# The first two projections of a two-layer encoder on unnormalised tokens, with the norm's scale in the weights and the tokens' factors at eviction

## The chip, the cores and the metric

The kernel runs on one core of one Trainium2 chip. A core has a matrix engine (TensorE; PE in the rows, and PEld for its weight loads), a vector engine (VectorE, DVE), an engine for functions and scaled copies (ScalarE, ACT), a general engine (GpSimd, POOL) and SyncE (SP), whose queue issues the DMAs here. The metric is the device time of one execution in microseconds (us).

## The reference

A trunk of two layers on 256 tokens of 1024 channels, all float32. Each layer has a token mixer and a SwiGLU FFN, with an RMSNorm before and behind each. The part that matters here:

```python
h = rms_norm(x, ln_mix_pre[l])          # x * rsqrt(mean(x*x) + eps) * gain
proj = h @ w_in[l]                      # one combined input projection
c_q, c_kv, k_pe, conv_u, r_q, r_k, r_v, r_g, gate_logits = jnp.split(proj, points, axis=-1)
y_mla = mla_branch(c_q, c_kv, k_pe, cos_m, sin_m, ...)   # norms c_q, c_kv; rotates k_pe
y_conv = conv_branch(conv_u, ...)                         # gated, width 31
y_ret = retention_branch(r_q, r_k, r_v, r_g, cos_r, sin_r, ...)
...                                     # gates, output projection, FFN
```

The first group of columns (c_q, c_kv and k_pe: 416 columns) is called the latents below; the first 512 columns of r_v are the values.

## The kernel before

**Split products.** A float32 product is made of three products of a faster format: each operand is split into a high part (a rounded copy, by ScalarE) and a low part (the rest, by VectorE), and high x high, high x low and low x high are added up in one bank. `split` does it for activations, `wunit` for a weight unit: one DMA of 416 or 512 KB into a buffer `raw` (5 of them), a copy into `whi` (9 buffers) on ScalarE (line 175), a subtraction into `wlo` (8 buffers) on VectorE (line 177). `mm3` (lines 186 to 188) issues the three products. A group of columns has four units of 256 rows each; `tok_mm` runs a unit over one block of 128 tokens (there are two), `feat_group` makes transposed outputs for both blocks at once.

**The start.** SP issues the norm's gain (one row), x block 0, two weight units, x block 1, and further units (lines 119, 120, 166, 393). Ten warm products on zeros run on TensorE meanwhile, and four instructions (line 131) that spread the gain row over 128 partitions in two banks. `first_norm` squares and sums a block (ScalarE one half, VectorE the other; lines 279, 280), POOL makes the factor rs (lines 142, 143), VectorE multiplies the tokens by rs and by the gain (line 264), TensorE transposes the normed block (line 270, two times four transposes) and `split` makes its high and low parts (lines 182, 183): the tile hT. Only then does the first product of the latents start.

**What follows.** Latents and values, each over both blocks (banks `pas` and `pvs`); the values are split at eviction into vrh and vrl. `setup_tables` makes sines and cosines of the positions (sinT, cosT) and the decay logarithms (lgt), mostly on VectorE, in buffers of the tag `half`, of which there are seven. `columns` transposes small parameter rows (prow, grow). `latent` norms a block's latents (lines 443 to 450, into cn) and rotates the key part into kpad (lines 378 to 383), which needs the tables; its inner function transposes cn and kpad on TensorE (lines 460, 461). Meanwhile TensorE goes on with the conv projections, four feature groups of 48 products each.

**What sets the order.** Each engine runs its instructions in a fixed list. The list is made when the program is built: a scheduler places ready instructions by priority (the order of the code) and its own estimate of times; waits between engines are semaphores. Nothing is reordered on the chip.

```python
def wunit(src, k, c):
    ...
    raw = wraw(src, k, c)[:, :n]
    S.copy(hi, raw)
    V.tensor_sub(lo, raw, hi.bitcast(F32))
```

Of the kernel before, what the change touches and what calls it, by code (L numbers as in the profile page):

```python
# [8 lines left out]
F32 = mybir.dt.float32  # L9
# [7 lines left out]
P = 128  # L17
# [9 lines left out]
NHI = 9  # L27
NLO = 8
NRAW = 5
WARM = 10  # L30
FFN = 2816
FT = FFN // P
EPS = 1e-6
# [25 lines left out]
def tile_hybrid_encoder(  # L59
# [44 lines left out]
    def mid(name):  # L104
        return act.tile([P, 1024], F32, tag="mid", name=name, bufs=5)
# [4 lines left out]
    def acc():  # L110
        return pacc.tile([P, 512], F32, tag="acc", name="acc")

    def tp():
        return ptp.tile([P, 512], F32, tag="tp", name="tp")


    xs = cst.tile([P, NB, D], F32, tag="xs", name="xs")
    grow1 = mid("grow1")
    nc.sync.dma_start(grow1[0:1, :], ln_mix_pre[0:1, :])
    nc.sync.dma_start(xs[:, 0, :], x[0, 0:P, :])  # L120
    ones = cst.tile([1, P], F32, tag="ones", name="ones")
# [4 lines left out]
    gfirst = [acc() for _ in range(2)]  # L126
# [37 lines left out]
    def wraw(src, k, c):  # L164
        raw = wp.tile([P, 1024], F32, tag="raw", name="raw", bufs=NRAW)
        nc.sync.dma_start(raw[:, :k * c].rearrange("p (k c) -> p k c", k=k),
                          src.rearrange("(k p) c -> p k c", p=P))
        return raw

    def wunit(src, k, c):  # L170

        n = k * c
        raw = wraw(src, k, c)[:, :n]
        hi = hi_tile()[:, :n]
        S.copy(hi, raw)  # L175
# [81 lines left out]
        duals.append(t)  # L257
        return t[:, :, :SEQ], t[:, :, SEQ:]

    def pre_norm(b, hn, ss, gain, hT):  # L260
        rs = sm.tile([P, 1], F32, tag="rs", name="rs")
        rsqrt_sum(rs, ss)
# [11 lines left out]
        return transposes  # L274

    def first_norm(b, gain, hT):
        hn = mid("hn")
        ss = sm.tile([P, 2], F32, tag="ss2", name="ss2")
        S.activation(hn[:, :512], xs[:, b, :512], AF.Square, scale=1.0 / 32.0, accum_out=ss[:, 0:1])
        V.scalar_tensor_tensor(hn[:, 512:], xs[:, b, 512:], 1.0 / D, xs[:, b, 512:],  # L280
                               op0=ALU.mult, op1=ALU.mult, accum_out=ss[:, 1:2])
        pre_norm(b, hn, ss, gain, hT)()

    def boundary(b, banks, gpost, gpre, hT):

# [102 lines left out]

    def a_unit(win, i):
        return wunit(win[2 * i * P:(2 * i + 2) * P, C_A:C_CONV], 2, C_CONV)  # L390
    first_norm(0, gfirst, hT)
    ua = [a_unit(w_in[0], i) for i in range(2)]
    nc.sync.dma_start(xs[:, 1, :], x[0, P:2 * P, :])
    first_norm(1, gfirst, hT)

    for l in range(DEPTH):
        win = w_in[l]


        if l == 0:  # L400
# [3 lines left out]
        uv = [wunit(win[2 * i * P:(2 * i + 2) * P, C_RV:C_RV + 512], 2, 512) for i in range(4)]  # L404

        gqkv = half("gqkv")[:, :QR + KVR]
        nc.sync.dma_start(gqkv[:, :QR], mla_q_norm[l].partition_broadcast(P))
# [57 lines left out]
                      pc[:, :3 * P].rearrange("p (j n) -> p j n", j=3))  # L465
            return f

        pas = [acc() for _ in range(NB)]
        pvs = [acc() for _ in range(NB)]
        for c, b in ((0, 0), (0, 1), (1, 0), (1, 1)) if l == 0 else ((0, 0), (1, 0), (0, 1), (1, 1)):  # L470
# [508 lines left out]
```

## Time and profile before

| | |
|---|---|
| three runs | 936.09, 936.37 (median), 939.99 us |
| profiled execution | 939.36 us, span of its rows 937.0 us |
| TensorE busy | 925.5 us, 99% of the span |
| VectorE busy | 694.5 us, 74% |
| ScalarE busy | 535.1 us, 57% |

Rows of the timeline give start, busy time of the row, engine, line, operation, the shape of the output and input, and the count; in brackets the idle time ahead of the row on its engine and what ended it. Products are pipelined: one of 0.35 us can start every 0.188 us, so that a price is read from start to start. The page's line PEclk, and the column PEclk of the windows, give the share of full clock (2.4 GHz) that was granted; 0.50 is 1.2 GHz.

### The profile page before, as it was taken

The numbers are of one execution on the slowest core, as the hardware profiler recorded it, in microseconds if no ns is written. First come the engines' busy times: TensorE is split into PE (matmuls) and PEld (weight loads), VectorE is DVE, ScalarE is ACT, GpSimd is POOL, SyncE is SP. The second block draws the span as 40 slices with busy tenths as digits, with TensorE's granted clock in tenths as the row PEclk, the third lists the DMA queues.
The fourth block names the chain that finished last, engine by engine and source line by source line (L and its number), as shares of the span: only waits on it lengthen the run. The fifth ranks groups of instructions, "written<-read, shape, count | busy, mean of one in ns | idle before, by whom it ended". The sixth has DMA issues, their size and how long they took to land.

```text
span 937.0 us, 13295 instructions
## 1 busy us (share of the span) xinstructions
PE 925.5 (99%) x4924; PEld 787.9 (84%) x4924; DVE 694.5 (74%) x1101; ACT 535.1 (57%) x821; POOL 35.9 (4%) x77
## 2 busy tenths in 40 slices
PE   8999999999999999999999999999999999999997
PEld 6999878888887888888889998788888888888885
DVE  6789999996658776664486899999766677667532
ACT  5775886544545666553365758755454555666431
POOL 1000000000010000000120000010000100000000
PEclk7999999999999999999999999999999999999999
DMA  6785455566636766565366655645755376666621
GB/s 226 245 254 160 147 163 179 144 194 181 182 91 236 252 182 191 193 198 187 98 203 199 197 152 166 196 135 162 197 172 179 125 233 200 194 182 185 203 85 45
DMA packets 113214, 166.70 MB, mean 178 GB/s; under 512 B 5929, under 2 KB 62905, under 8 KB 113150
## 3 DMA queue, kind: packets, MB, share of 16 engines
q1 hardware_dynamic: 113150, 165.87, 57.8%
q8 instruction: 38, 0.62, 0.3%
q14 instruction: 26, 0.21, 0.1%
HBM read 164.80 MB, written 1.05 MB: 177 GB/s over the span
## 4 chain that ended last, share of the span: by engine, by line
PE 94%; ACT 2%; DVE 2%; DMA 1%; issue 0%; POOL 0%; DVEq 0%; SPq 0%; POOLq 0%; ACTq 0%
PE acc L186 22%; PE acc L188 22%; PE acc L187 22%; PE acc L241 13%; PE acc L239 7%; PE acc L238 2%; PE tp L613 1%; PE tp L649 1%; DMA raw<-in_ffn_w_up_dram 1%; PE tp L638 1%; PE tp L679 1%; DVE wlo L177 1%; PE tp L270 1%; ACT whi L175 1%; ACT qT L564 0%; DMA raw<-in_w_in_dram 0%
## 5 line engine op out<-in xcount | busy, mean ns | idle before, releaser
L175 ACT CAST whi<-raw 128x1024 fp32r<-128x1024 f32 (+1 forms) x300 | 312.2, 1049 | 226.9 <-PE acc L188 133.4
L177 DVE TENSOR_TENSOR wlo<-raw,whi 128x1024 fp32r<-128x1024 f32 (+1 forms) x300 | 362.6, 1216 | 106.0 <-PE acc L187 60.6
L241 PE MATMUL acc<-hT,whi 128*128 128x512 f32 x504 | 179.8, 397 | 0.0
L186 PE MATMUL acc<-whi,hT 128*128 128x512 f32 (+1 forms) x416 | 168.2, 404 | 0.4 <-ACT hT L182 0.4
L188 PE MATMUL acc<-whi,hT 128*128 128x512 f32 (+1 forms) x416 | 162.6, 391 | 1.0 <-DVE hT L183 0.8
L187 PE MATMUL acc<-wlo,hT 128*128 128x512 f32 (+1 forms) x416 | 162.4, 390 | 0.0
L239 PE MATMUL acc<-hT,wlo 128*128 128x256 f32 x576 | 149.1, 279 | 0.0
L239 PEld LDWEIGHTS acc<-hT,wlo 128*128 128x128 f32 x576 | 108.7, 189 | 6.2
L241 PEld LDWEIGHTS acc<-hT,whi 128*128 128x128 f32 x504 | 94.8, 188 | 19.5
L521 DVE SCALAR_TENSOR_TENSOR cacc<-apad,ccol,cacc 128x256 f32<-128x256 f32 x240 | 108.0, 476 | 1.3
L188 PEld LDWEIGHTS acc<-whi,hT 128*128 128x128 f32 x416 | 78.7, 189 | 18.7 <-DVE hT L183 2.8
L186 PEld LDWEIGHTS acc<-whi,hT 128*128 128x128 f32 x416 | 78.9, 190 | 17.9 <-issue 3.1
L187 PEld LDWEIGHTS acc<-wlo,hT 128*128 128x128 f32 x416 | 79.0, 190 | 13.7
L186 PE MATMUL acc<-hT,whi 128*128 128x256 f32 x256 | 73.5, 287 | 0.5 <-ACT kT L564 0.5
L188 PE MATMUL acc<-hT,wlo 128*128 128x256 f32 x256 | 72.5, 283 | 0.0
L187 PE MATMUL acc<-hT,whi 128*128 128x256 f32 x256 | 72.5, 283 | 0.0
L186 PE MATMUL acc<-whi,hidh 128*128 128x512 f32 x176 | 68.6, 390 | 0.0
L188 PE MATMUL acc<-whi,hidl 128*128 128x512 f32 x176 | 68.6, 389 | 0.0
L187 PE MATMUL acc<-wlo,hidh 128*128 128x512 f32 x176 | 68.5, 389 | 0.0
L186 PEld LDWEIGHTS acc<-hT,whi 128*128 128x128 f32 x256 | 49.1, 192 | 1.5 <-ACT kT L564 1.4
L187 PEld LDWEIGHTS acc<-hT,whi 128*128 128x128 f32 x256 | 49.1, 192 | 0.1
L188 PEld LDWEIGHTS acc<-hT,wlo 128*128 128x128 f32 x256 | 49.1, 192 | 0.0
(236 smaller groups left out, 1269.0 us busy)
## 6 DMA issues: line engine op xcount, KB each, us to landing
raw<-in_w_in_dram SPq DMA_DIRECT2D x112, 512.0 KB, 4.2
raw<-in_ffn_w_gate_dram SPq DMA_DIRECT2D x44, 512.0 KB, 4.5
raw<-in_ffn_w_up_dram SPq DMA_DIRECT2D x44, 512.0 KB, 4.5
raw<-in_ffn_w_down_dram SPq DMA_DIRECT2D x44, 512.0 KB, 4.6
raw<-in_ret_w_o_dram SPq DMA_DIRECT2D x16, 512.0 KB, 3.7
raw<-in_w_out_dram SPq DMA_DIRECT2D x16, 512.0 KB, 3.5
raw<-in_mla_w_o_dram SPq DMA_DIRECT2D x8, 512.0 KB, 4.7
raw<-in_conv_w_pw_dram SPq DMA_DIRECT2D x8, 512.0 KB, 3.4
```

Source lines behind the costliest of these rows:

```text
L175: S.copy(hi, raw)
L177: V.tensor_sub(lo, raw, hi.bitcast(F32))
L186: T.matmul(o, lh, rh, start=start, stop=False)
L187: T.matmul(o, lh, rl, start=False, stop=False)
L188: T.matmul(o, ll, rh, start=False, stop=stop)
L238: T.matmul(ps, wh, both[:, k, :], start=True, stop=False)
L239: T.matmul(ps[:, SEQ:], wl, both[:, k, :SEQ], start=False, stop=False)
L241: T.matmul(ps, wh, both[:, k, :], start=False, stop=k == KT - 1)
L270: T.transpose(ps[:, j * P:(j + 1) * P], hn[:, (4 * c + j) * P:(4 * c + j + 1) * P], ident)
L521: V.scalar_tensor_tensor(cacc[:, j, :], src, ccol[:, j, w:w + 1], cacc[:, j, :], op0=ALU.mult, op1=ALU.add)
L613: T.matmul(ps[:, j * SEQ:(j + 1) * SEQ], qT[:QK, 2 * pr + j, b * P:(b + 1) * P], kT[:QK, 2 * pr + j, :], start=True, stop=True)
L638: T.transpose(pt[:, jk * P:(jk + 1) * P], pe[:, jk * P:(jk + 1) * P], ident)
```

## The change

The first two groups of layer 0 (latents and values) take the tokens as they are. Since the norm is x times a factor per token times a gain per channel, the gain can go into the weights' rows and the factor into the output's rows. `g8` loads the gain as 8 rows of 128, one transpose makes of it eight columns `pcol`. `plain_T` transposes raw tokens and splits them into the tile `u` (uTh, uTl). `scaled_unit` stands for `wunit`: ScalarE copies each of the unit's two row blocks with a scale per partition, VectorE makes the low part with one fused operation each. The latents' banks are copied to `sa` with the token's factor, and the values are multiplied by it when they are split. The old norm with hT is still made, for all that follows, now with a broadcast gain tile and behind the values' splits. `Line` chains the instructions of the start on TensorE, ScalarE and VectorE in the order of the code. WARM goes from 10 to 7, and one warm product (`keep_busy(1)`) stands later.

```diff
-WARM = 10
+WARM = 7
...
-    grow1 = mid("grow1")
-    nc.sync.dma_start(grow1[0:1, :], ln_mix_pre[0:1, :])
     nc.sync.dma_start(xs[:, 0, :], x[0, 0:P, :])
-    ones = cst.tile([1, P], F32, tag="ones", name="ones")
-    V.memset(ones, 1.0)
+    g8 = act.tile([KT, P], F32, tag="grow", name="g8")
+    nc.sync.dma_start(g8, ln_mix_pre[0].rearrange("(k p) -> k p", p=P))
...
-    for i in range(WARM):
-        T.matmul(pw, warm[:, :P], warm, start=True, stop=True)
-        if i == 3:
-            for c in range(2):
-                T.matmul(gfirst[c], ones, grow1[0:1, c * 512:(c + 1) * 512], start=True, stop=True)
+    def keep_busy(n):
+        for _ in range(n):
+            inPE(T.matmul(pw, warm[:, :P], warm, start=True, stop=True))
+    keep_busy(WARM)
...
+    def plain_T(b, c, u):
+        ps = tp()
+        for j in range(4):
+            inPE(T.transpose(ps[:, j * P:(j + 1) * P], xs[:, b, (4 * c + j) * P:(4 * c + j + 1) * P], ident))
+        hi, lo = (t[:, 4 * c:4 * c + 4, b * P:(b + 1) * P] for t in u)
+        pv = ps.rearrange("p (j n) -> p j n", j=4)
+        inACT(S.copy(hi, pv))
+        return lambda: inDVE(V.tensor_sub(lo, pv, hi.bitcast(F32)))
+
+    def scaled_unit(src, k0, c, col, line=True):
...
+        for k in range(2):
+            inACT(S.activation(hi[:, k, :], raw[:, k, :], AF.Copy, scale=col[:, k0 + k:k0 + k + 1]))
+        for k in range(2):
+            inDVE(V.scalar_tensor_tensor(lo[:, k, :], raw[:, k, :], col[:, k0 + k:k0 + k + 1],
+                                         hi[:, k, :].bitcast(F32), op0=ALU.mult, op1=ALU.subtract))
+        return hi, lo
...
-    first_norm(0, gfirst, hT)
-    ua = [a_unit(w_in[0], i) for i in range(2)]
-    nc.sync.dma_start(xs[:, 1, :], x[0, P:2 * P, :])
-    first_norm(1, gfirst, hT)
+    def fast_first(pas):
+        pg = tp()
+        inPE(T.transpose(pg[:, :KT], g8, ident[:KT, :KT]))
+        col = act.tile([P, KT], F32, tag="gcol", name="pcol")
+        inDVE(V.tensor_copy(col, pg[:, :KT]))
...
+        def products(i, b, what):
+            o = pas[b][:, :C_CONV]
+            for k in range(2):
+                t = u[what == "lh"][:, 2 * i + k, b * P:(b + 1) * P]
+                inPE(T.matmul(o, t, units[i][what == "hl"][:, k, :], start=i == 0 and k == 0 and what == "hh",
+                              stop=i == 3 and k == 1 and what == "hl"))
+        lo = plain_T(0, 0, u)
+        lo()
+        unit(0)
+        lo = plain_T(0, 1, u)
+        lo()
+        nc.sync.dma_start(xs[:, 1, :], x[0, P:2 * P, :])
+        keep_busy(1)
+        products(0, 0, "hh")
+        products(0, 0, "lh")
+        for c in range(2):
+            plain_T(1, c, u)()
+        products(0, 0, "hl")
+        for what in ("hh", "lh", "hl"):
+            products(0, 1, what)
+        for i in range(1, 4):
+            unit(i)
+            for b in range(NB):
+                for what in ("hh", "lh"):
+                    products(i, b, what)
+            for b in range(NB):
+                products(i, b, "hl")
+        return u, col
...
         if l == 0:
-            ua += [a_unit(win, i) for i in range(2, 4)]
+            uT, pcol = fast_first(pas)
+            uv = [scaled_unit(win[2 * i * P:(2 * i + 2) * P, C_RV:C_RV + 512], 2 * i, 512, pcol) for i in range(4)]
+            gain = gain_tile(ln_mix_pre[0])
+            first = [first_norm(b, gain, hT) for b in range(NB)]
...
+        if l == 0:
+            for b in range(NB):
+                sa = half("sa")[:, :C_CONV]
+                S.activation(sa, pas[b][:, :C_CONV], AF.Copy, scale=factors[b])
+                pas[b] = sa
+            for i in range(4):
+                for b in range(NB):
+                    tok_mm(pvs[b], uT, b, 2 * i, uv[i], 2, i == 0, i == 3)
+                if i % 2:
+                    first[i // 2]()
+            for b in range(NB):
+                vh, vl = vrh[:, b, :512], vrl[:, b, :512]
+                S.activation(vh, pvs[b], AF.Copy, scale=factors[b])
+                V.scalar_tensor_tensor(vl, pvs[b], factors[b], vh.bitcast(F32), op0=ALU.mult, op1=ALU.subtract)
```

**The order on the engines.** ScalarE at the very start; numbers behind names count the tiles. Before:

```order
L279 ACTIVATE hn_112,ss2_113<-xs_73 128x512 [waits DMAHW1_49]
L175 CAST whi_137<-raw_135 128x832 [waits DMAHW2_49]
L175 CAST whi_143<-raw_141 128x832 [waits DMAHW3_49]
L279 ACTIVATE hn_148,ss2_149<-xs_73 128x512 [waits DMAHW4_49]
L175 CAST whi_173<-raw_171 128x832 [waits DMAHW5_49]
L182 CAST hT_111<-tp_121 128x4x128 [waits PE_49]
L182 CAST hT_111<-tp_128 128x4x128 [waits PE_49]
```

After:

```order
L296 CAST uTh_111<-tp_113 128x4x128 [waits PE_49]
L305 ACTIVATE whi_122<-raw_120,pcol_109 128x416 [waits DMAHW2_49,DVE_49]
L305 ACTIVATE whi_122<-raw_120,pcol_109 128x416
L296 CAST uTh_111<-tp_128 128x4x128 [waits PE_49]
L296 CAST uTh_111<-tp_141 128x4x128 [waits PE_49]
L296 CAST uTh_111<-tp_148 128x4x128 [waits PE_49]
L305 ACTIVATE whi_165<-raw_163,pcol_109 128x416 [waits DMAHW4_49]
```

The square of the norm has gone from the head of the list; a copy of transposed raw tokens and the first unit's two scaled copies stand there.

VectorE behind the values' splits (wlo with the highest numbers are units of the conv projections; ang is the first tile of the tables). Before, from the last value unit on:

```order
L183 TENSOR_TENSOR hT_111<-tp_164,hT_111 128x4x128 [waits Activation_49]
L177 TENSOR_TENSOR wlo_193<-raw_189,whi_191 128x1024 [waits DMAHW0_49]
L177 TENSOR_TENSOR wlo_199<-raw_195,whi_197 128x1024 [waits DMAHW1_49,Activation_49]
L177 TENSOR_TENSOR wlo_205<-raw_201,whi_203 128x1024 [waits DMAHW2_49,Activation_49]
L334 CAST pos_337<-pos_i_327 128x2 [waits DMAHW2_49]
L337 CAST ang_339<-pos_r_329 128x256 [waits DMAHW3_49]
L338 TENSOR_SCALAR ang_339<-ang_339,inv_331 128x256 [waits DMAHW4_49,DVE_49]
```

After, from the second conv group's last unit on:

```order
L187 TENSOR_TENSOR wlo_562<-raw_558,whi_560 128x1024 [waits DMAHW4_49,Activation_49]
L193 TENSOR_TENSOR hT_102<-tp_357,hT_102 128x4x128 [waits Activation_49]
L193 TENSOR_TENSOR hT_102<-tp_364,hT_102 128x4x128 [waits Activation_49]
L559 SCALAR_TENSOR_TENSOR vrl_288<-acc_106,rs_270,vrh_287 128x512
L372 CAST ang_387<-pos_r_377 128x256 [waits DMAHW7_49,DMAHW1_49,PE_49]
L375 TENSOR_SCALAR ang_387<-inv_379,pos_385 128x16 [waits DMAHW1_49]
L373 TENSOR_SCALAR ang_387<-ang_387,inv_379 128x256 [waits DMAHW0_49,DVE_49]
```

The tables' first operation has moved behind four conv units, the low parts of hT and both value evictions, and it now waits for TensorE too.

TensorE at the transposes of the rotary key (kpad) of block 0. Before, in the second feature group (bank acc_516):

```order
L186 MATMUL acc_516<-hT_111,whi_506 128x256
L187 MATMUL acc_516<-hT_111,whi_506 128x256
L188 MATMUL acc_516<-hT_111,wlo_508 128x256
L461 MATMUL tp_496<-ident_96,kpad_109 96x128 [waits DVE_49]
L186 MATMUL acc_516<-hT_111,whi_506 128x256
```

After, in the third feature group (bank acc_635):

```order
L196 MATMUL acc_635<-hT_102,whi_631 128x256 [waits Activation_49]
L197 MATMUL acc_635<-hT_102,whi_631 128x256
L539 MATMUL tp_544<-ident_87,kpad_100 96x128 [waits DVE_49]
L198 MATMUL acc_635<-hT_102,wlo_633 128x256
L539 MATMUL tp_589<-ident_87,kpad_100 96x128 [waits DVE_49]
```

The transposes of the rotary key have moved behind more products: 54 of the conv projections stood ahead of the first before and 72 ahead of the second, 110 and 111 stand there now.

## Rows read from the trace of the kernel before

**Rows 1.** the page's part 1: busy time, share of the span, instructions

```profile
PE 925.5 (99%) x4924; PEld 787.9 (84%) x4924; DVE 694.5 (74%) x1101; ACT 535.1 (57%) x821; POOL 35.9 (4%) x77
```

**Rows 2.** waits of TensorE over the run: us in total, times, longest

```profile
PE tp L270 <- DVE hn L264: 1.8, 2, 1.6
...
```

**Rows 3.** timeline of the start: tokens, norm, transposes, first product

```profile
1.13 0.36 SPq L120 DMA_DIRECT2D xs<-in_x_dram  x1
...
4.83 0.63 ACT L279 ACTIVATE hn<-xs 128x512 f32<-128x512 f32 x1 [2.83 <-DMA xs<-in_x_dram]
...
8.52 1.97 PE L270 MATMUL tp<-ident,hn 128*128 128x128 f32 x8 [1.56 <-DVE hn L264]
...
10.88 0.72 PE L186 MATMUL acc<-whi,hT 128*128 128x416 f32 x1 [0.39 <-ACT hT L182]
```

**Rows 4.** windows: stretch, length, each engine's busy time, clock, DMA, GB/s

```profile
1.30:7.00 5.70, 5.66 (x14) 1.75 (x14) 0.92 (x3) 2.39 (x5) 1.67 (x8) 1.00 0.88 296
7.00:8.50 1.50, 0.00 (x0) 0.00 (x0) 1.50 (x3) 0.89 (x2) 0.00 (x0) 0.64 1.01 397
8.50:10.80 2.30, 1.97 (x8) 1.57 (x8) 2.30 (x5) 1.98 (x5) 0.00 (x0) 0.50 1.05 402
10.80:17.60 6.80, 6.40 (x20) 5.49 (x21) 6.08 (x8) 3.98 (x7) 1.50 (x2) 0.50 0.78 276
17.60:35.30 17.70, 17.70 (x86) 15.77 (x85) 13.99 (x42) 10.27 (x19) 1.93 (x4) 1.00 0.60 191
```

**Rows 5.** timeline of ScalarE and VectorE: copies, low parts, splits, tables

```profile
5.87 0.89 ACT L175 CAST whi<-raw 128x832 fp32r<-128x832 f32 x1 [0.32 <-DMA raw<-in_w_in_dram]
...
17.50 0.59 ACT L182 CAST hT<-tp 128x512 fp32r<-128x512 f32 x1 [0.61 <-PE tp L270]
...
18.12 0.69 DVE L183 TENSOR_TENSOR hT<-tp,hT 128x512 fp32r<-128x512 f32 x1 [0.51 <-ACT hT L182]
18.73 3.49 DVE L177 TENSOR_TENSOR wlo<-raw,whi 128x1024 fp32r<-128x1024 f32 x3
...
26.14 0.45 DVE L345 SCALAR_TENSOR_TENSOR sinT<-tmp,ang 128x288 f32<-128x288 f32 x1
26.51 0.16 DVE L363 TENSOR_SCALAR lgt<-lgt 128x16 f32<-128x16 f32 x1
...
28.40 0.30 DVE L342 TENSOR_SCALAR tmp<-ang 128x288 f32<-128x288 f32 x1
28.62 0.17 DVE L366 TENSOR_TENSOR lgt<-lgt 128x16 f32<-128x16 f32 x1
28.70 0.34 DVE L450 SCALAR_TENSOR_TENSOR cn<-acc,rs,gqkv 128x128 f32<-128x128 f32 x1
```

**Rows 6.** timeline of TensorE at full clock: products, second key transpose

```profile
18.01 0.35 PE L188 MATMUL acc<-whi,hT 128*128 128x416 f32 x1
...
24.39 0.39 PE L186 MATMUL acc<-whi,hT 128*128 128x512 f32 x1
...
35.27 0.28 PE L186 MATMUL acc<-hT,whi 128*128 128x256 f32 x1
...
35.63 0.28 PE L186 MATMUL acc<-hT,whi 128*128 128x256 f32 x1
...
45.36 0.27 PE L461 MATMUL tp<-ident,kpad 128*96 128x128 f32 x1
```

**Rows 7.** chain of waits: eight transposes at full clock (start, us, what)

```profile
742.14 0.87 PE tp L270 x8
```

**Rows 8.** timeline of POOL: the two steps of one factor

```profile
23.40 0.23 POOL L138 TENSOR_SCALAR rs<-ss 128x2 f32<-128x2 f32 x1 [10.97 <-ACT cn L444]
23.71 0.71 POOL L139 TENSOR_TENSOR rs<-rs,nhalf 128x2 f32<-128x2 f32 x1
```

**Rows 9.** timeline of ScalarE: a table load and what follows

```profile
30.64 1.28 ACT L351 ACT_TABLE_LOAD   x1
31.93 0.45 ACT L351 ACTIVATE sinT<-sinT 128x288 f32<-128x288 f32 x1
```

More of the change, by code (lines that the diff above doesn't have):

```diff
@@ L117, in tile_hybrid_encoder, with __init__, __call__ @@
     xs = cst.tile([P, NB, D], F32, tag="xs", name="xs")
-    grow1 = mid("grow1")
-    nc.sync.dma_start(grow1[0:1, :], ln_mix_pre[0:1, :])
     nc.sync.dma_start(xs[:, 0, :], x[0, 0:P, :])
-    ones = cst.tile([1, P], F32, tag="ones", name="ones")
-    V.memset(ones, 1.0)
+    g8 = act.tile([KT, P], F32, tag="grow", name="g8")
+    nc.sync.dma_start(g8, ln_mix_pre[0].rearrange("(k p) -> k p", p=P))
+    class Line:
+        def __init__(self):
+            self.last = None
+        def __call__(self, ins):
+            if self.last is not None:
+                tc.add_manual_dep(ins.ins, self.last, mybir.DependencyInfo(
+                    mybir.DependencyClass.NoSync, mybir.DependencyReason.DATA), reason="order")
+            self.last = ins.ins.name
+    inPE, inACT, inDVE = Line(), Line(), Line()
     warm = act.tile([P, 512], BF16, tag="half", name="warm", bufs=7)
@@ L125, in tile_hybrid_encoder @@
     pw = tp()
-    gfirst = [acc() for _ in range(2)]
-    for i in range(WARM):
-        T.matmul(pw, warm[:, :P], warm, start=True, stop=True)
-        if i == 3:
-            for c in range(2):
-                T.matmul(gfirst[c], ones, grow1[0:1, c * 512:(c + 1) * 512], start=True, stop=True)
+    def keep_busy(n):
+        for _ in range(n):
+            inPE(T.matmul(pw, warm[:, :P], warm, start=True, stop=True))
+    keep_busy(WARM)
     ident = cst.tile([P, P], F32, tag="ident", name="ident")
@@ L258, in new_hT, with pre_norm @@
         return t[:, :, :SEQ], t[:, :, SEQ:]
-    def pre_norm(b, hn, ss, gain, hT):
+    def pre_norm(b, hn, ss, gain, hT, first=False):
         rs = sm.tile([P, 1], F32, tag="rs", name="rs")
+        if first:
+            factors.append(rs)
         rsqrt_sum(rs, ss)
@@ L274, in pre_norm @@
         return transposes
+    def plain_T(b, c, u):
[7 more added lines that the diff above has]
+    def scaled_unit(src, k0, c, col, line=True):
+        raw = wraw(src, 2, c).rearrange("p (k c) -> p k c", k=2) if c == 512 else \
+            wraw(src, 2, c)[:, :2 * c].rearrange("p (k c) -> p k c", k=2)
+        hi, lo = (t[:, :2 * c].rearrange("p (k c) -> p k c", k=2) for t in (hi_tile(), lo_tile()))
+        for k in range(2):
[4 more added lines that the diff above has]
+        return hi, lo
     def first_norm(b, gain, hT):
@@ L278, in first_norm @@
         ss = sm.tile([P, 2], F32, tag="ss2", name="ss2")
[L279 to L282, printed above, removed]
+        inACT(S.activation(hn[:, :512], xs[:, b, :512], AF.Square, scale=1.0 / 32.0, accum_out=ss[:, 0:1]))
+        inDVE(V.scalar_tensor_tensor(hn[:, 512:], xs[:, b, 512:], 1.0 / D, xs[:, b, 512:],
+                                     op0=ALU.mult, op1=ALU.mult, accum_out=ss[:, 1:2]))
+        return pre_norm(b, hn, ss, [gain[:, cs] for cs in halves()], hT, True)
     def boundary(b, banks, gpost, gpre, hT):
@@ L390, in a_unit, with unit @@
         return wunit(win[2 * i * P:(2 * i + 2) * P, C_A:C_CONV], 2, C_CONV)
-    first_norm(0, gfirst, hT)
-    ua = [a_unit(w_in[0], i) for i in range(2)]
-    nc.sync.dma_start(xs[:, 1, :], x[0, P:2 * P, :])
-    first_norm(1, gfirst, hT)
+    def fast_first(pas):
[3 more added lines that the diff above has]
+        inDVE(V.tensor_copy(col, pg[:, :KT]))
+        u = [big(n, F32R).rearrange("p (k n) -> p k n", k=KT) for n in ("uTh", "uTl")]
+        units = []
+        def unit(i):
+            units.append(scaled_unit(w_in[0][2 * i * P:(2 * i + 2) * P, C_A:C_CONV], 2 * i, C_CONV, col))
+        def products(i, b, what):
[26 more added lines that the diff above has]
+        return u, col
@@ L396, in tile_hybrid_encoder @@
+    factors = []
     for l in range(DEPTH):
         win = w_in[l]
+        pas = [acc() for _ in range(NB)]
+        pvs = [acc() for _ in range(NB)]
         if l == 0:
-            ua += [a_unit(win, i) for i in range(2, 4)]
+            uT, pcol = fast_first(pas)
+            uv = [scaled_unit(win[2 * i * P:(2 * i + 2) * P, C_RV:C_RV + 512], 2 * i, 512, pcol) for i in range(4)]
+            gain = gain_tile(ln_mix_pre[0])
+            first = [first_norm(b, gain, hT) for b in range(NB)]
         else:
@@ L403, in tile_hybrid_encoder @@
             ua = [a_unit(win, i) for i in range(4)]
-        uv = [wunit(win[2 * i * P:(2 * i + 2) * P, C_RV:C_RV + 512], 2, 512) for i in range(4)]
+            uv = [wunit(win[2 * i * P:(2 * i + 2) * P, C_RV:C_RV + 512], 2, 512) for i in range(4)]
         gqkv = half("gqkv")[:, :QR + KVR]
@@ L466, in latent @@
             return f
-        pas = [acc() for _ in range(NB)]
-        pvs = [acc() for _ in range(NB)]
-        for c, b in ((0, 0), (0, 1), (1, 0), (1, 1)) if l == 0 else ((0, 0), (1, 0), (0, 1), (1, 1)):
+        if l == 0:
[12 more added lines that the diff above has]
+                V.scalar_tensor_tensor(vl, pvs[b], factors[b], vh.bitcast(F32), op0=ALU.mult, op1=ALU.subtract)
+        for c, b in () if l == 0 else ((0, 0), (1, 0), (0, 1), (1, 1)):
             for i in range(4):
```

## The prediction

> **What bounds the kernel now.** I read the page's first two parts, then the waits of TensorE, the windows of the first 50 us and the timeline there. TensorE is busy for 925.5 of 937.0 us [rows 1], and over the whole run no other engine makes it wait for more than 1.8 us in all, for the normed tokens at the start [rows 2]. So after the start only two things shorten this kernel: an earlier start of the stream of products, and less TensorE work. The diff touches nothing behind the conv projections: from some 60 us on every engine's order is that of before. What counts is by how much TensorE comes earlier to one and the same product in that stretch.
>
> In the first 17.6 us two things cost time. The first real product starts at 10.88 [rows 3], behind norm, scaling and transposes. And TensorE's granted clock, full up to 7 us, falls in the stretch 7.0 to 8.5, where TensorE has nothing, to half (1.2 GHz) and stays there until 17.6 [rows 4]. From 17.6 to 35.3 it never waits [rows 4].
>
> **Against which time.** The profiled execution took 939.36 us: span 937.0 and 2.36 around it. The median of the runs shown is 936.37, which is 3.0 lower, but one of those runs took 939.99. I make the sum against 939.36 and deal with the 3.0 us at the end.
>
> **Part 1, the start.** The token DMA is issued first instead of second, one issue (0.4 us) earlier, so x lands at about 4.4 instead of 4.83 [rows 3]. Eight transposes at half clock take 1.97 [rows 3]: the first four end at 5.4 and the rest at 6.4. The fixed order on ScalarE is then a copy (0.59 for 512 columns [rows 5]) to 6.0, and two scaled copies of 416 columns. These are not in the trace; 512 columns take 0.59 and 832 take 0.89 [rows 5], so I take 0.5 each, ending at 6.5 and 7.0. The first product starts at 6.6, not 10.88: 4.3 us earlier. The norm (square, sum, POOL, two multiplications) no longer stands ahead of it.
>
> **Part 2, TensorE's work up to the conv projections.** At full clock a 416-column product comes every 0.188 us (34 of them from 18.01 to 24.39) and a 512-column product every 0.227 (48 of them from 24.39 to 35.27) [rows 6]; eight transposes take 0.87 [rows 7]. Unit 0 of the latents (12 products) and the second block's 8 transposes, paced by ScalarE's copies, end at about 10.1. 36 products more: 6.8, to 16.9. The 48 value products: 10.9, to 27.8. New are 16 transposes of the normed rows, since the raw tokens are transposed too: 1.74, to 29.6. Against 35.27 in the trace that is 5.7 us earlier, and the five small transposes of columns (0.4) are then done too. The two ones-row products (four instructions) and three warm products go, but stood in idle time.
>
> **Part 3, what is late next.** The normed transposed tokens (hT) were ready long before; now they are needed at 29.6, and their making stands behind all the scaled splits on VectorE. I follow that queue. The value weights come in order at 400 GB/s [rows 4]; the fourth unit waits behind a new 512 KB gain broadcast and lands at about 17.5. Its split on VectorE ends at 19.4, the statistics of both blocks at 20.8, POOL's two steps take 1.0 from start to end [rows 8] and 0.1 for the hand-over, the four multiplications at 0.61 end at 23.9. Then, at 1.14 for a weight split and 0.61 for 512 columns, from start to start [rows 5]: two splits 26.3; hT low parts of block 0 27.5; three small ones 27.9; two more splits, with one value eviction between, 30.9; low parts of block 1 at 31.5 and 32.1. So VectorE, not TensorE, sets the first conv product: 31.3, the gain is then 35.27 + 0.4 - 31.3 = 4.4.
>
> Next come the rotary tables. Before, they were made from 22.1 on, beside the value products. The new order has them behind block 1's last eviction: their buffer is the one that the transposed parameter rows leave, and those transposes now stand behind all the value products. Their prices from start to start: 0.37 for a fused operation on 288 columns, 0.22 for a plain one, 0.08 for a small one, 1.14 for a split [rows 5]. Eviction to 32.75; thirteen operations, 2.1, to 34.85; a wait for block 0's latent statistics, which on ScalarE now stand behind three weight casts (to 36.3); latent 0 complete at 37.4; nine operations with one split, 2.65, to 40.05; latent 1 at 41.0; sixteen with one split, 3.65, to 44.65 (the cosine is then in ScalarE's hands for 0.45, under the next split); that split and the twelve last operations, to 46.9. Then the rotary key is ready to be transposed.
>
> TensorE wants latent 0 after 49 products of 0.12 [rows 6], at 37.2 (0.2 late), latent 1 23 products on (0.5 late), the keys 38 products on, at 45.9 (1.1 late with both). It goes on at 47.05, behind 111 products. In the trace before, 72 products stood ahead of the second key's transpose at 45.36 [rows 6]; the 111th ends 39 x 0.12 later, at 50.07. **Gain: 3.0 us**, to 936.4 against 939.36. Half of what the start gains is given back to VectorE.
>
> The other edits. The scaled splits do the same columns as the plain ones, two fused operations for one plain. One of 512 lies between 0.57 (half a split) and 0.66 (0.37 by 512/288); I take 0.6, since the fourth unit waits for its DMA anyway, and 0.1 on the chain at most. The two evictions of latents (0.5 each) stand on ScalarE at 21 to 23, ahead of the conv splits, which VectorE reaches no sooner. The gain broadcast is not in the trace at this place; if it lands 2 us later than the 400 GB/s say, the whole chain is up to 1 later, and if the fourth unit isn't held up at all, 0.8 earlier. Two more table loads on ScalarE take 1.28 each, and the operation behind one starts at its end (30.64 + 1.28, next at 31.93) [rows 9]; they end at 44.1, just before the cosine arrives. The Trainium skill ("ScalarE: Activation LUTs", What ACT_TABLE_LOAD costs) puts a drain of about 1.38 beside each load; the trace shows none, and by the rule the keys would come 2 us later and the kernel at 938.4. I go by the row.
>
> **Rivals.**
> (a) *The clock falls again.* Between 4.3 and 8.6 TensorE does mostly transposes and waits, as before between 7 and 10.8, where it was at half clock throughout although it was busy with transposes for 1.97 of 2.3 us [rows 4]. If it falls at 7.4 and rises at 17.6 as before, 416 columns at 1.2 GHz take 0.35 instead of 0.188: some 24 of 48 are done by then, the rest end at 22.2, the value products and transposes at 35.1, the first conv product is at 35.7 and, with the same vector chain behind it, the 111th ends at 50.4: 939.7, slower than the median run by 3.3. A rise 3.4 earlier would give 938.6. It decides from the point where TensorE's last transpose comes behind 31.3. For it: the same kind of stretch lost the clock before. Against it: the new stream has no idle time as long as 1.5 us, one warm product stands in it, and products start by 7. The Trainium skill ("TensorE: Matmul & The Clock Gate", Part 4: PE-mode transpose) says that full clock does not engage for transposes, which is on this rival's side; no row here separates it from the idle time around them.
> (b) *VectorE keeps up.* If its waits are shorter than I reckon and the tables come in time, TensorE's own sum holds: 29.6, the 111th product at 43.9, 6.2 us gained, 933.2. For it: VectorE is busy for only 13.99 of 17.7 us up to 35.3 [rows 4]. Against: the new order has four more low parts and two more splits ahead of the keys.
> (c) *The change hardly does what it says:* the median runs of before never paid the 3.0 us of half clock, so that the earlier start only replaces products at full clock: 936.4, no gain against 936.37.
>
> **The numbers.** The 3.0 us between the profiled execution and the median: if they lie in something that both kernels share, my sum becomes 936.4 - 3.0 = 933.4; if they are the half clock, which the new kernel escapes in every run, it stays 936.4. The run at 939.99 and the size (17 products at 0.16 us more each are 2.7) speak for the second, but nothing shows that the half clock was absent in the others. I take the middle, 934.9. Chances: my case 0.45; (a) 0.2; (b) 0.2, at 930.2 to 933.2 by the same offset; (c) 0.15. The range runs from 931.0, (b) near its lower end, to 939.5, (a) without the offset. What a measurement can tell from no change is 0.5%, 4.7 us: faster means below 931.7, which only (b) with the whole offset gives: 0.14. Slower means above 941.0, (a) with a later table or gain on top: 0.06. Within: 0.80.
>
> **What would show it.** In the profile after: the first product at 6.5 to 7.1; granted clock full from some 4 us on (wrong: 0.5 anywhere between 7 and 18); the value products done at 27 to 29; a wait of TensorE for VectorE's hT at 29 to 32; then short waits for cn and kpad, the last at about 47, with VectorE nearly without a gap from 20 to 47. If TensorE has no waits behind 30 us, (b) holds. If the 111th conv product ends behind 49, the sum is wrong, and the windows say whether clock or tables did it.

## The result and the profile after

The changed kernel takes 949.79 us (median; 948.85 to 950.97), before 936.31 beside it: a ratio of 1.0129, interval 1.0109 to 1.0149. It is 13.5 us slower, where I had forecast 934.9 and a range up to 939.5. The profiled execution took 950.2 us, span 948.3. The two profiled executions lie 10.8 us apart, not 13.5, because that of before took 3 us longer than its median; the traces below compare these two. The page's busy time answers to [rows 1]: TensorE has 6.6 us more for 11 instructions more, which suggests that its products themselves have become dearer.

```profile
PE 932.1 (98%) x4935; PEld 787.5 (83%) x4935; DVE 699.4 (74%) x1113; ACT 543.1 (57%) x837; POOL 37.7 (4%) x77
```

The longest of TensorE's waits over the whole run (us in total, times, longest), beside [rows 2]:

```profile
PE tp L282 <- DVE hn L276: 2.7, 1, 2.7
PE acc L196 <- ACT qT L654: 1.7, 2, 1.2
PE acc L443 <- ACT whi L305: 1.0, 1, 1.0
PE tp L539 <- DVE kpad L418: 0.7, 1, 0.7
```

All of its waits add up to 9.3 us, 4.5 more than before: they don't explain 13. To see where the rest goes I set the two traces beside each other product by product. From 50 us of before on TensorE's order is the same, and products are counted from the program's end; the first two columns match a value product and a conv product by their place among the others of their kind. The table gives the time in before and how much later the same product comes in the changed kernel (a minus: earlier).

| before, us | 31.4 | 46.3 | 59.4 | 73.7 | 171 | 288 | 554 | 735 | 926 |
|---|---|---|---|---|---|---|---|---|---|
| later by, us | -0.5 | 2.4 | 3.5 | 6.9 | 6.9 | 7.9 | 8.6 | 9.6 | 11.3 |

So 6.9 us are lost up to 74 us, and 4.4 more, little by little, where TensorE hardly waits. The start itself came as forecast, as TensorE's timeline shows; against [rows 3] the first product is 4.0 us earlier:

```profile
6.84 0.99 PE L443 MATMUL acc<-whi,uTh 128*128 128x416 f32 x2 [0.98 <-ACT whi L305]
...
8.65 1.09 PE L293 MATMUL tp<-ident,xs 128*128 128x128 f32 x8 [0.44 <-DMA xs<-in_x_dram]
...
18.41 0.40 PE L196 MATMUL acc<-whi,uTh 128*128 128x512 f32 x1
...
26.90 1.32 PE L282 MATMUL tp<-ident,hn 128*128 128x128 f32 x8 [2.73 <-DVE hn L276]
...
35.21 1.03 PE L282 MATMUL tp<-ident,hn 128*128 128x128 f32 x8
```

The windows, with the columns of [rows 4], show the clock: full from 4.25 on, and half twice, each time behind a stretch in which TensorE had waited.

```profile
4.25:10.80 6.55, 4.97 (x28) 3.25 (x27) 3.51 (x7) 3.69 (x7) 0.00 (x0) 1.00 1.00 344
10.80:17.60 6.80, 6.80 (x36) 6.71 (x37) 5.15 (x9) 4.05 (x8) 0.00 (x0) 1.00 1.02 279
...
24.00:28.20 4.20, 1.46 (x10) 1.05 (x10) 2.90 (x8) 1.19 (x4) 2.87 (x4) 1.00 0.38 99
28.20:31.60 3.40, 3.40 (x10) 2.63 (x9) 3.32 (x5) 3.40 (x6) 0.00 (x0) 0.50 1.06 374
...
72.50:76.00 3.50, 3.36 (x15) 2.87 (x14) 2.02 (x6) 3.44 (x6) 0.00 (x0) 0.51 0.89 296
```

Why was hn late? SyncE's timeline: the gain broadcast stands ahead of three of the four value units, the second is issued at 9.79 and the last two from 13.13 on (before, all four were out by 12.0). The queue's waits show that a DMA issue of this program also waits for the DMA eight places ahead of it: the second of these two waited 1.3 us for the gain to land, as the last row says (us in total, times, longest).

```profile
4.54 1.12 SPq L258 DMA_DIRECT2D gain<-in_ln_mix_pre_dram  x1
...
9.79 0.38 SPq L176 DMA_DIRECT2D raw<-in_w_in_dram  x1
...
13.13 2.17 SPq L176 DMA_DIRECT2D raw<-in_w_in_dram  x2
```

```profile
SPq L176 <- DMA gain<-in_ln_mix_pre_dram: 1.3, 1, 1.3
```

The second, third and fourth unit land at 19.1, 20.5 and 21.8. So ScalarE's casts of them begin at 19.08, and VectorE, with nothing else allowed in its fixed order, is idle for 3.9 us before 19.84. Statistics, hn, the first table operation (38.66; in before 22.20) and the last of the key (53.29; the prediction had 46.9) follow from there. ScalarE, then VectorE:

```profile
19.08 4.05 ACT L305 ACTIVATE whi<-raw,pcol 128x512 fp32r<-128x512 f32 x6 [4.24 <-DMA raw<-in_w_in_dram]
```

```profile
19.84 4.19 DVE L307 SCALAR_TENSOR_TENSOR wlo<-raw,pcol,whi 128x512 fp32r<-128x512 f32 x6 [3.89 <-ACT whi L305]
23.94 0.69 DVE L315 SCALAR_TENSOR_TENSOR hn<-xs 128x512 f32<-128x512 f32 x1
...
38.66 0.28 DVE L372 CAST ang<-pos_r 128x256 f32<-128x256 int32 x1
...
53.29 0.17 DVE L418 TENSOR_TENSOR kpad<-kpad,tk 128x16 f32<-128x16 f32 x1
```

### The profile page after: what moved, and what is told of

Same layout as the page of the kernel before. It is cut to its first block, busy times and chain, and to the rows that moved or that the text cites. A ratio compares the mean times of both kernels' runs of the same rounds, so it can differ in the third digit from the quotient of the medians.

```text
span 948.3 us, 13349 instructions
## 1 busy us (share of the span) xinstructions
PE 932.1 (98%) x4935; PEld 787.5 (83%) x4935; DVE 699.4 (74%) x1113; ACT 543.1 (57%) x837; POOL 37.7 (4%) x77
## 3 DMA queue, kind: packets, MB, share of 16 engines
HBM read 165.32 MB, written 1.05 MB: 175 GB/s over the span
## 4 chain that ended last, share of the span: by engine, by line
PE 92%; DMA 2%; DVE 2%; ACT 2%; issue 0%; POOL 0%; SPq 0%; DVEq 0%; POOLq 0%; ACTq 0%
PE acc L196 21%; PE acc L197 21%; PE acc L198 21%; PE acc L251 12%; PE acc L249 7%; PE acc L248 2%; PE tp L703 1%; DMA raw<-in_w_in_dram 1%; PE tp L739 1%; PE tp L728 1%; PE tp L769 1%; DVE wlo L187 1%; DMA xs<-in_x_dram 1%; PE tp L282 1%; ACT qT L654 0%
## 5 line engine op out<-in xcount | busy, mean ns | idle before, releaser
L185 ACT CAST whi<-raw 128x1024 fp32r<-128x1024 f32 (+1 forms) x292 | 304.8, 1051 | 225.5 <-PE acc L198 141.1
L187 DVE TENSOR_TENSOR wlo<-raw,whi 128x1024 fp32r<-128x1024 f32 (+1 forms) x292 | 354.4, 1221 | 107.8 <-PE acc L197 65.5
L196 PE MATMUL acc<-whi,hT 128*128 128x512 f32 (+1 forms) x384 | 155.0, 404 | 0.0
L198 PE MATMUL acc<-whi,hT 128*128 128x512 f32 (+1 forms) x384 | 149.7, 390 | 0.3 <-DVE hT L193 0.3
L197 PE MATMUL acc<-wlo,hT 128*128 128x512 f32 (+1 forms) x384 | 149.4, 389 | 0.0
L196 PEld LDWEIGHTS acc<-whi,hT 128*128 128x128 f32 x384 | 72.2, 188 | 16.5 <-issue 3.1
L198 PEld LDWEIGHTS acc<-whi,hT 128*128 128x128 f32 x384 | 72.1, 188 | 16.2 <-DVE hT L193 1.1
L197 PEld LDWEIGHTS acc<-wlo,hT 128*128 128x128 f32 x384 | 72.2, 188 | 13.2
```

What stands on the lines that cost most here:

```text
L196: T.matmul(o, lh, rh, start=start, stop=False)
L197: T.matmul(o, lh, rl, start=False, stop=False)
L198: T.matmul(o, ll, rh, start=False, stop=stop)
```

## The experiments

**First set: four suspects, one at a time.** Theory A: a new small tile, `pcol` (32 bytes a partition, in the pool that also holds hT and the tiles `big`, `mid` and `half`), moves the `big` and `mid` tiles 32 bytes off multiples of 512 bytes (of the `big` ones the first lies at byte 152,096 of a partition, which leaves 32; in before at 173,056, which leaves 0; hT and the `half` tiles stay at multiples), and products that read them come at a wider spacing.

e1_align takes `pcol` out of that pool; each engine's order stays as in the changed kernel.

```diff
-        col = act.tile([P, KT], F32, tag="gcol", name="pcol")
+        col = sm.tile([P, KT], F32, tag="pcol", name="pcol", bufs=1)
```

> The changed kernel with one edit: the 32-byte tile of gain columns lies in another pool, so that the large activation tiles (hid, onT, mT and others, 8 KB a partition each) start again at multiples of 512 bytes instead of 32 bytes behind one. The order of instructions on every engine stays the same. Theory A (the position of the stationary operand sets the spacing): the FFN's last projection falls from 232 to 235 ns a product back to 227, and the time to 944 to 946 us (4 to 6 below 949.8). Rival B (the wider spacing comes from other traffic at that time, or from the earlier delay): the spacing stays at 232 to 235 and the time at 949 to 951.

e2_before_shift does the reverse: the kernel before with an unused tile of 32 bytes ahead of the `big` ones, which alone of the tiles at multiples of 512 it moves; the order on each engine stays here too.

```diff
     hT = new_hT()
+    pad = act.tile([P, 8], F32, tag="pad", name="pad")
+    G.memset(pad, 0.0)
```

> The kernel before with one edit: an unused 32-byte tile is placed ahead of the large activation tiles, which moves them 32 bytes off their multiple of 512. Theory A: the products of the FFN's last projection go from 227 to 232 to 235 ns, the time to 940 to 942 us (4 to 6 above 936.3). Rival B: 227 ns and 936 to 937 us.

Measured: e1 945.04 us, ratio to before 1.0086 (1.0071 to 1.0101); e2 941.48, 1.0047 (1.0030 to 1.0063). TensorE's busy time falls to 926.3 us in e1 and rises to 932.0 in e2. The page's group of down-projection products (count, busy us, mean ns of one) in the changed kernel, in e1 and in e2:

```profile
L196 PE MATMUL acc<-whi,hidh 128*128 128x512 f32 x176 | 69.7, 396 | 0.0
```

```profile
L196 PE MATMUL acc<-whi,hidh 128*128 128x512 f32 x176 | 68.6, 390 | 0.0
```

```profile
L186 PE MATMUL acc<-whi,hidh 128*128 128x512 f32 x176 | 69.7, 396 | 0.0
```

The price is the spacing. In the changed kernel nine products take 2.10 us from start to start, 0.233 each; in before nine take 2.04, 0.227. TensorE's timeline of the changed kernel, then of before:

```profile
904.75 0.40 PE L196 MATMUL acc<-whi,hidh 128*128 128x512 f32 x1
...
906.85 0.40 PE L196 MATMUL acc<-whi,hidh 128*128 128x512 f32 x1
```

```profile
897.84 0.39 PE L186 MATMUL acc<-whi,hidh 128*128 128x512 f32 x1
...
899.88 0.39 PE L186 MATMUL acc<-whi,hidh 128*128 128x512 f32 x1
```

With e1 the lag against before no longer grows: 7.05 us at 74, 6.4 at 926. With e2 it grows from 0.2 at 241 to 3.5 at 901. A is shown from both sides; it is worth 4.8 us by the medians of e1 and the changed kernel, 4.0 by their ratios to before, and 4.4 in e2. Products whose stationary tile is hT, at a multiple of 512 in both kernels, keep their spacing (0.227 at 700 us); where the moved tile is the moving operand (cT, 256 columns, from 64.8 us of the changed kernel on), the spacing is no wider either (0.118, in before 0.120). So it is the stationary operand's place that counts here, hidh and its like.

e3_order lets SyncE issue the value units ahead of the gain broadcast (theory C: the late value units cause the wait for hn).

```diff
+        d = nc.sync.dma_start(raw[...], ...)      # also: gain, gqkv, prow
+        if starting:
+            inSP(d)                               # a fixed order on SyncE
```

> The changed kernel, with SP made to issue the value units ahead of the gain broadcast, the latents' gains and the parameter rows. Theory C (the early loss begins with the value weights, which land behind the broadcasts at 19 to 20.5 us): the last value unit lands at 17 or before, VectorE's gap between 15 and 19.8 shrinks to under 2, the first conv product comes 3 us earlier and the time is 943 to 947 us. Rival D (VectorE's queue is the limit by its own work): the first conv product moves by under 1 us and the time stays at 948.5 to 950.

Measured: 950.25 us, 1.0141 (1.0126 to 1.0156), no gain. It doesn't decide: with these loads fixed, the scheduler put the positions' load and its cast on VectorE ahead of the second block's low parts, and these waited for a DMA of 1 KB. TensorE lost 2.0 us there, after 2.0 us for the first unit's copy (1.0 in the changed kernel); the clock was half from 7.6 to 11.0, from 14.4 to 17.85 and from 58.8 to 62.2. The copies of the last value unit began at 22.3, no earlier than in the changed kernel (21.8). VectorE's row, then TensorE's waits:

```profile
13.26 0.17 DVE L374 CAST pos<-pos_i 128x2 f32<-128x2 int32 x1 [3.69 <-DMA pos_i<-in_positions_dram]
```

```profile
PE acc L448 <- DVE uTl L302: 2.0, 1, 2.0
PE acc L448 <- ACT whi L310: 2.0, 1, 2.0
```

e4_tables gives the inverse frequencies and the decay logits tiles of their own (theory D: the tables wait for a buffer that the parameter rows leave).

```diff
-        inv = half("inv")[:, :HR + 1]
+        inv = cst.tile([P, 32], F32, tag="inv", name="inv")[:, :HR + 1]
-        lgt = half("lgt")
+        lgt = cst.tile([P, 96], F32, tag="lgt", name="lgt")
```

> The changed kernel with two small setup tiles (the inverse frequencies and the decay logarithms) in the constant pool instead of the seven shared half buffers, so that the rotary tables needn't wait for the buffer of the parameter rows. Theory D (the tables' place behind hT on VectorE costs the time): the rotary key is ready 4 us or more earlier than 53.4, the waits for cn and kpad go, and the time is 945 to 948 us. Theory C: the value weights land as late as in the changed kernel, hT is ready at 36 to 38 as before, and the time falls by 1 us at most (948.5 to 950).

Measured: 946.59 us, 1.0106 (1.0089 to 1.0122), 3.2 us less than the changed kernel (2.2 by the ratios). The first table operation comes at 30.8 instead of 38.7, the key is done at 48.3 instead of 53.5, and TensorE's waits for kpad and cn are gone. From 79 us on e4 is 3.1 us ahead of the changed kernel, evenly. So the edit is worth this much, but only a small part of it is won at the keys: at 59.4 e4 is 0.5 us ahead. The other 2.6 come at the queries, whose copies on ScalarE begin at 66.1 instead of 68.5: TensorE waits 0.6 us for them instead of 1.7, and no half clock follows. D is shown as a cause; its way to the end is longer than I had expected. The wait for hn stays (3.4 us). VectorE of e4:

```profile
30.77 0.29 DVE L372 CAST ang<-pos_r 128x256 f32<-128x256 int32 x1
...
48.14 0.17 DVE L418 TENSOR_TENSOR kpad<-kpad,tk 128x16 f32<-128x16 f32 x1
```

**Second set: what is left with A and D mended.** f1_both has both edits, e1's and e4's. f2_stats moves one line of it, and with it the value units' loads behind the gain's:

```diff
-            uv = [scaled_unit(...) for i in range(4)]
             gain = gain_tile(ln_mix_pre[0])
             first = [first_norm(b, gain, hT) for b in range(NB)]
+            uv = [scaled_unit(...) for i in range(4)]
```

f3_loads fixes SyncE's order for all loads of the start: latent units, value units, gain, then the small ones (e3 without its fault). f4_stats_loads has the fixed loads and the statistics ahead of the value splits.

> The changed kernel with the column tile in a pool of its own (so that the 1024- and 2048-column tiles start on multiples of 512 bytes again) and with tiles of their own for the inverse frequencies and the decay logits (so that VectorE need not wait with the tables for the buffer of the parameter rows). If the two losses are independent, 4.8 and 3.1 us go: 949.8 - 7.9 = 941.9. If the late tables had already been paid for by other waits, less than the sum: 943.5 or more. In both cases the wait of TensorE for hn, about 3 us at 24 to 28, and half clock behind it stay, and some 3 us remain to the profiled execution of before, 5.6 to its median.

> As f1_both, but the first block norm (squares, sums and the two multiplications by factor and gain) stands ahead of the splits of the value weights in ScalarE's and VectorE's fixed order. Theory B, the place of the norm in the fixed order: VectorE is idle from 15.0 to 19.8 in the changed kernel, so the norm goes there, the wait for hn (2.7 to 3.4 us) goes, half clock at 28 to 31.6 with it (up to 1.7 us), and the time is f1_both less 3 to 5 us, 937 to 939. Rival, theory C, the value weights are late because small loads and the gain broadcast stand ahead of them: the norm's 2.8 us of VectorE only move, the split of the last value unit ends no earlier, and the time stays within 1 us of f1_both.

> As f1_both, but SyncE issues all four value units ahead of the gain broadcast, the parameter rows and the tables' data. Theory C: the value weights land at 14.5 to 17.5 instead of 19.0 to 20.5, the splits and the norm behind them end up to 3 us earlier, and the time is f1_both less 2 to 4 us, 938 to 940. Rival, theory B: with the norm still behind the splits, and the gain landing later, hn comes no more than 1 us earlier and the time stays within 1 us of f1_both.

> As f1_both, with both: the statistics ahead of the value splits, and the value units ahead of all small loads on SyncE. If B and C each hold a part, this is the fastest of the four: TensorE no longer waits for hn, the clock stays full behind 4 us, and the time is 934 to 937, level with before. If it is no faster than the better of f2_stats and f3_loads, the two are one and the same wait. If all four stay above 940, neither the norm's place nor the loads explain what is left, and the cause lies behind 36 us (tables, keys, queries).

| kernel | us | ratio to before, interval | wait for hn, us |
|---|---|---|---|
| f1_both | 942.55 | 1.0058, 1.0040 to 1.0076 | 3.3 |
| f2_stats | 942.63 | 1.0058, 1.0042 to 1.0074 | 0.3 |
| f3_loads | 942.03 | 1.0050, 1.0034 to 1.0066 | 1.0, in two |
| f4_stats_loads | 943.48 | 1.0065, 1.0049 to 1.0080 | 0.2 |

A and D add up (941.9 expected). B and C both take most of the wait for hn away, as expected of each, and neither gains anything, nor do both together in f4, where I had expected 934 to 937: my prices for them were wrong. In f2 TensorE is 4.2 us ahead of before at the value product of 31.4, and 2.3 behind at 46.3. It stands still in between, as its row shows; on ScalarE (second fence) the first conv cast waits for its weights until 29.36, the latents' statistics stand behind it, and the second block's hT, transposed only behind the last value product, comes at 36.05. The wait had only moved, and half clock stands behind it (36.4 to 39.9; in f3 and f4 from 37 to 44).

```profile
36.45 0.66 PE L538 MATMUL tp<-ident,cn 128*128 128x128 f32 x2 [3.76 <-DVE cn L526]
```

```profile
29.36 1.05 ACT L185 CAST whi<-raw 128x1024 fp32r<-128x1024 f32 x1 [3.94 <-DMA raw<-in_w_in_dram]
...
36.05 1.07 ACT L192 CAST hT<-tp 128x512 fp32r<-128x512 f32 x2
```

**Third set: the next waits in turn.** g1_early is f2 with the transposes moved; g2_early_loads has them too, with loads in the order latent units, gain, value units, the rest.

```diff
-                if i % 2:
-                    first[i // 2]()
+                if i == 0:
+                    first[0]()
+                if i == 1:
+                    first[1]()
```

> As f2_stats, but TensorE transposes the normed rows of the first block behind the first value unit and those of the second behind the second, instead of behind the second and the fourth. Theory G: in f2_stats and f3_loads the value products end 2 to 4 us ahead of before, and then stand still because the second block is transposed only behind the last of them, so that its copies and low parts lie bare on the path, behind weight casts and tables. Then the first conv product comes at 31 to 33 instead of 36 to 40, and the time falls from 942.6 to 938 to 940. Rival H: the conv weights arrive at 29 in f2_stats, because SyncE issues them at 23 behind the small loads, and ScalarE and VectorE idle for them; then TensorE waits for the weights' splits instead, and the time stays within 1 us of 942.6.

> As g1_early, with the loads in a fixed order: latent units, gain broadcast, value units, and only then the small loads and the conv units. Theory G and C together: hn is ready ahead of the second value unit, the value weights land at 15 to 19, and the time is 936 to 939, level with before. Rival H: the conv weights come no earlier than in f4_stats_loads (31 us), TensorE waits for their casts at 31 to 36 and the time stays at 941 to 944.

Measured: g1 943.06 us, 1.0046 (1.0030 to 1.0063); g2 941.00, 1.0028 (1.0014 to 1.0043), with before at 938.53 in that comparison. Early transposes alone gain 0.12% by the ratios, within the intervals, where G expected 0.3 to 0.5%, and rival H holds for g1; with the loads in order there is a gain, but not to level. In g2's trace (938.50 us) TensorE is 3.5 us ahead of before at 31.4, 1.3 ahead at 59.4 and 0.4 behind at 73.7. ScalarE and then TensorE at that place:

```profile
62.02 1.05 ACT L191 CAST whi<-raw 128x1024 fp32r<-128x1024 f32 x1 [1.48 <-DMA raw<-in_w_in_dram]
63.28 1.05 ACT L191 CAST whi<-raw 128x1024 fp32r<-128x1024 f32 x1 [0.22 <-DMA raw<-in_w_in_dram]
64.23 2.41 ACT L663 ACTIVATE qT<-acc 64x512 f32<-64x512 f32 x4
```

```profile
65.48 0.50 PE L202 MATMUL acc<-whi,cT 128*128 128x512 f32 x1 [0.98 <-ACT qT L663]
```

The copies of the queries stand behind casts of weights that aren't needed yet and that the DMA, busy at a share of 0.96 to 1.04 from 50 to 60 us, delivers no earlier than in before (qT at 63.78 there). A lead of TensorE ends at that queue. g6_q_first moves the copies ahead of the last four of these casts; g7_again is g2 once more, beside it.

```diff
...
+            if count[0] > 4:           # casts of the rotated queries' and keys' weights
+                inQ(one)               # a fixed order: behind the copies of qT and kT
...
```

> As g2_early_loads, but ScalarE has the copies of the queries (qT) ahead of the last four weight casts of the rotated queries and keys, instead of behind three of them. Theory I: in g2_early_loads TensorE is 1.29 us ahead of before up to 59 us and 0.43 behind it from 74 on, because the copies stand on ScalarE behind casts that wait for weights which the DMA delivers no earlier than in before (DMA share 0.96 to 1.04 from 50 to 60). Then the copies come at 62 to 63 instead of 64.23, the lead of 1.3 us stays, and the time falls by 1.2 to 1.7 us against g7_again: level with before or up to 0.1% below. Rival J: TensorE reaches the queries no sooner, and the casts that are now later hold up the rotated queries at 70 to 74: within 0.5 us of g7_again.

> The kernel of g2_early_loads once more, beside g6_q_first on the same chip. It gives the difference to g6 and a second reading of the ratio to before. Theory: 1.0028 again within its interval (1.0014 to 1.0043), 0.3% slower than before, 1.0% faster than the changed kernel. Rival: the ratio was low only because before ran at 938.5 in that comparison; then it is 1.005.

Measured: g6 937.54 us, 1.0006 (0.9996 to 1.0016); g7 940.10, 1.0029 (1.0016 to 1.0041), the ratio of g2 again. g6 takes 2.6 us less than g7 (2.2 by the ratios), more than the 1.2 to 1.7 expected, and is level with before. The expected lead wasn't there: g6's trace has TensorE 1.9 us behind before at 59.4, and the copies come at 64.87, not at 62 to 63. But from there to 73.7 it gains 0.6 us on before, where g2 and g7 lose 1.7 and 1.3, and ScalarE's copy now waits for the product, not for a weight. So theory I is shown; why the gain is larger than its price is not:

```profile
64.87 1.20 ACT L668 ACTIVATE qT<-acc 64x512 f32<-64x512 f32 x2 [2.06 <-PE acc L209]
```

Together the steps lead from 1.0129 to 1.0086 (A), 1.0058 (D), 1.0028 (statistics, loads and transposes) and 1.0006 (queries). No version beat before.

## Why the prediction was wrong

- **What bounds the kernel** was read rightly from [rows 1, 2], but not the conclusion: "What counts is by how much TensorE comes earlier to one and the same product in that stretch." This is the step that failed first: it put every loss behind 60 us at nothing. TensorE's order there is indeed that of before, but 3.4 us more are lost at the queries (59 to 74 us), and 4.4 by wider spacing. I had counted the change's instructions, not its tiles: 32 bytes cost more than any instruction that it adds. The premise ("every engine's order is that of before") was wrong too: ScalarE's order is the same only from 71 us on, since a weight cast now stands between the two pairs of query copies, and VectorE's from 140 on. f1_both has the same order on ScalarE and loses 0.1 us between 59 and 74, so the order alone isn't the price: in the changed kernel the four casts from 61.87 on wait 3.6 us for their weights, TensorE waits 1.7 for the copies behind them, and half clock follows, which takes another 1.7. ScalarE before, then in the changed kernel:

```profile
63.78 2.42 ACT L564 ACTIVATE qT<-acc 64x512 f32<-64x512 f32 x4
```

```profile
67.55 1.06 ACT L185 CAST whi<-raw 128x1024 fp32r<-128x1024 f32 x1 [1.12 <-DMA raw<-in_w_in_dram]
68.51 1.19 ACT L654 ACTIVATE qT<-acc 64x512 f32<-64x512 f32 x2
69.60 1.04 ACT L185 CAST whi<-raw 128x1024 fp32r<-128x1024 f32 x1
70.66 1.20 ACT L654 ACTIVATE qT<-acc 64x512 f32<-64x512 f32 x2
```

- **Part 1, the start**, was right: first product 6.84, forecast 6.6.
- **Part 2, TensorE's own work**: the values begin at 18.4 instead of 16.9, because unit 0 with block 1's transposes ends at 11.6 instead of 10.1 (0.4 us of it a wait for block 1); the 36 products behind it take 6.8, as forecast. The values end at 35.2 instead of 27.8: besides that 1.5, 2.7 us of waiting for hn, 1.1 for eight transposes that I had put behind them, and half clock from 28.2 to 31.6, where a product comes every 0.43 us instead of 0.23. That the value weights are there in time was taken from the 400 GB/s of [rows 4], which hold there only up to 10.8; for 10.8 to 17.6 the same rows have 276, at a DMA share of 0.78. Now it was 279 in that stretch, at a share of 1.02.
- **Part 3, VectorE's chain** had the right mechanism and the wrong sizes. The fourth unit, forecast at 17.5, landed at 21.8; statistics ended at 25.2 instead of 20.8; the second block's low parts at 38.1 instead of 32.1, the key at 53.5 instead of 46.9. I had let VectorE work without a gap from 17.5 on; its fixed order held it idle for 3.9 us ahead of 19.84, with the statistics ready to be made behind. The second key's transpose came at 53.54, where before is at 50.07 behind as many products: 3.5 us later, not 3.0 earlier. These 6.5 us, the 3.4 at the queries and the 4.4 of spacing make up the miss of the profiled execution (950.2 against the sum's 936.4) but for 0.5 us. That the tables wait for the buffer of the parameter rows stood in the prediction; that giving them tiles of their own saves 3 us, most of it at the queries, e4 showed.
- **Table loads**: 1.28 us without a drain, as [rows 9] had it: a load at 44.62, the next work at 45.92.
- **Rival (a)**, the clock falling at 7.4, did not come in the changed kernel's trace: the granted clock is 1.00 from 4.25 to 28, with sixteen transposes of the tokens between 4.55 and 9.74. The Trainium skill ("TensorE: Matmul & The Clock Gate", Part 4: PE-mode transpose) has full clock not engage for transposes; with products and a warm product around them, these rows show it kept. Where the clock did fall, TensorE had waited, 2.7 us before 26.9 and 1.7 us in two waits between 69 and 72. In the traces of e3 and g6, where TensorE waited 2.0 us for the first unit, it was 0.50 from 7.6 to 11: there (a) came in part. So (a) named the right price, and in the changed kernel at the wrong place. (By its own terms its transposes end at 34.8, not 35.1, which changes nothing in it.)
- **Rivals (b) and (c)** were both too kind. No rival had a loss behind 60 us, so the chance of slower, 0.06, came from the start alone. That the clock was "full up to 7 us" in before misreads [rows 4]: the trace's record of the clock begins at 4.0, and ahead of it the column says 1.00 by default, while seven warm products of 512 columns take 3.0 us from 1.3 on, 0.43 each, which is the spacing of 512 columns at half clock in the changed kernel's rows. So a column of 1.00 at the start proves nothing by itself. In e2, which has before's start, the record begins at 16.0, and up to there products of 416 columns come every 0.35 us. So no run shows that half clock makes up the 3.0 us that the prediction weighs in its sum, as (c) has it; what does stays open.

What stays open: why the 32 bytes widen the spacing (only this one offset was tried), and where the last of the lead goes: in g6's trace TensorE still waits 1.6 us for low parts of conv weights, with half clock behind it (38.4 to 41.8).

## What to carry over

Ask of a change not only what it makes each engine do, but where its tiles push the others: compare the addresses of the tiles that the longest loops read as stationary operands. An earlier start is worth only what the next fixed queue passes on; follow the lead through each of them (loads, casts, evictions) until it reaches a stretch that no load sets. When a wait goes and the time stays, look for the same microseconds some 10 us further on.

## What the runs showed of the hardware

- A stationary operand 32 bytes off a multiple of 512 bytes: 512-column products every 0.233 us instead of 0.227, in two kernels, with no wait in the trace (weight loads show 0.188 us in both). A moving operand at such a place: 256-column products every 0.118 us, against 0.120.
- Sixteen transposes among products and warm products ran at full clock, from 4.55 to 9.74 us of the changed kernel's trace; in e3 and g6 a wait of 2.0 us ahead of the first product was followed by half clock from 7.6 on.
- A 512 KB broadcast issued at 4.54 landed some 10 us later, and the loads around it ran at 279 GB/s from 10.8 to 17.6, at a DMA share of 1.02 (in before, weight units alone: 402 at 1.05 from 8.5 to 10.8).
